# Feed-forward stages: moving a subtraction from GpSimd to VectorE, a rounding from ScalarE to VectorE, and the convolution's input from SBUF to PSUM

## The chip, the cores and the metric

The kernel runs on one core of a Trainium2 chip. The metric is the device time of one execution in microseconds (us), the median over runs. The engines are named as in the profile: PE is TensorE's matmul, PEld its weight load, DVE is VectorE, ACT is ScalarE, POOL is GpSimd, and SP is SyncE, which here only issues loads.

## The reference

A sequence of 256 tokens of width 1024 goes through two transformer layers (an RWKV layer and a differential attention layer, each followed by a dense gated feed-forward) and then through a third block (token mixers with gated linear recurrences, followed by a convolutional gated feed-forward). What matters here are the three feed-forwards:

```python
def swiglu_ffn(h, w_gu, w_down):
    gate, up = jnp.split(h @ w_gu, 2, axis=-1)
    return (jax.nn.silu(gate) * up) @ w_down
...
def conv_ffn(h, w_up, taps, conv_b, w_down, rows):
    a, g = jnp.split(h @ w_up, 2, axis=-1)
    ...
    gc = lax.conv_general_dilated(g2, tp[:, :, None, :].astype(g.dtype), (1, 1), 'SAME', ...
    gc = gc.reshape(bsz, t, f) + conv_b
    return (a * jax.nn.gelu(gc, approximate=False)) @ w_down
```

The dense ones run twice, with 2816 hidden features each. The convolutional one has 2816 hidden features too; its gate branch is a 3x3 depthwise convolution over the 256 tokens seen as a grid of 4 rows of 64.

## The kernel before, in words

**Two-part numbers.** Every operand of a matmul is split into a rounded high part and a low part, `hi` (type fp32r) and `lo = raw - hi`, and each product is three matmuls: high by high, high by low, low by high (`mm3`). `split` (line 276) does this for a tile: ScalarE copies `raw` into `hi` with rounding (line 277), then an engine subtracts (`sub`, line 274). The subtraction runs on VectorE unless the caller names another engine.

**Weights.** `stream` (line 280) loads a weight tile of 128 x 1024 floats (512 KB) with a DMA on SP's queue (`fetch`, line 265) into a ring of five `raw` buffers, and splits it into rings of `hi` and `lo` buffers, three deep each for the up weights, and four deep for the down weights, which are called `dhi` and `dlo` in the profile.

**A feed-forward** (`ffn`) goes over 22 steps `fb` of 128 hidden features. In a step, two weight tiles (f = 0 and f = 1, the gate and the up half) are streamed and 48 matmuls of 256 columns write the two halves of one PSUM bank, which the profile names `p` in two steps and `tr` in the next two. Then `post(fb)` runs a hook that makes the hidden activation `raw` (tile name `act`, 128 x 256), splits it into `acth` and `actl`, and once enough steps are pending streams the down weight of an older step and issues its 12 matmuls of 512 columns into four `acc` banks. So a step has 60 matmuls: 48 and 12. With `lag=2` the down matmuls run two steps behind, and the last four steps' wait until the end (`tail=4`).

**Who subtracts.** The three feed-forwards pass `eng = lambda f: G if f else V` to `ffn`: the `lo` of the f = 0 tile is subtracted on VectorE, that of the f = 1 tile on GpSimd. `dlo` and `actl` are VectorE's.

**The hooks.** `silu_hook` (line 833): ScalarE's Silu of one half of the bank, VectorE's product with the other half (line 836). `conv_hook` (line 1261): ScalarE copies the gate half out of PSUM into a tile `gs` in SBUF (line 1263) and makes the centre tap from it (line 1265); VectorE adds the other eight taps one by one into `cacc` (line 1272), each reading `gs` and `cacc`; ScalarE applies Gelu (line 1274) and VectorE multiplies with the other half of the bank (line 1275).

**Beside the dense feed-forwards** run the modulation vectors of the third block (`ada_extra`): 48 more tiles of 512 KB (`wada`, two buffers, same SP queue), each multiplied and summed on VectorE against one or two rows (tile `junk`, line 856); 20 tiles are asked for in the first dense feed-forward and 28 in the second, and 16 of the 48 are used twice.

**Order.** The instructions of each engine are put in an order by a scheduler that works with its own estimates; each engine then runs its list strictly in that order. So an edit can move instructions far from it, and an instruction that waits holds up all that stand behind it on its engine, loads on SP included.

Of the kernel before, what the change touches and what calls it, by code (L numbers as in the profile page):

```python
# [17 lines left out]
T = 256  # L18
# [149 lines left out]
def body(ctx, tc, a, at):  # L168
# [35 lines left out]
        return scratch("s_" + s, (n + 7) // 8 * 8, 2)[:, :n]  # L204

    class FMt:
        """feature-major [1024, 256]: two tiles of 4 blocks of 128 features"""

        def __init__(self, pool, tag, dt=F32):
            self.t = [pool(tag, 1024, 2, dt) for _ in range(2)]  # L210
# [6 lines left out]
            return self.v[b][:, :, t * P:(t + 1) * P]  # L217

    def mark(*names):
        """the last instruction so far of each of these engines"""  # L220
        own = {getattr(mybir.EngineType, n) for n in names or ("Pool", "Activation", "DVE")}
        m = {}
        for i in reversed(nc.cur_bb.bb.instructions):
            if i.engine in own and i.engine not in m:
                m[i.engine] = i
                if len(m) == len(own):
                    break
        return m
# [26 lines left out]
    def C(n):  # L255
        o, w = at[n]
        return cst[:, o:o + w]
# [115 lines left out]

    def ptm(jobs, hid, lag=2, eng=lambda m: None, acc_bank=lambda: bank("p"),
            gain=None, ring=None):
        """jobs: (weights, first chunk, callback(t, psum)) of 512 output columns each"""
        xh, xl = hid
        steps = [(j, g) for j in range(len(jobs)) for g in range(4)]
        loaded, acc = {}, {}
        for i in range(len(steps) + lag):  # L380
            for t in range(2):
                m = i - lag * t
                if not 0 <= m < len(steps):
                    continue
                j, g = steps[m]
                w, c0, fin = jobs[j]
                if m not in loaded:
                    loaded[m] = stream(w, c0 + g, 2, eng(m), None if gain is None else gain[:, 2 * g:2 * g + 2],
                                       ring)
                wh, wl = loaded[m]  # L390
                if g == 0:
                    acc[j, t] = acc_bank()
                for k in range(2):
                    kk = 2 * g + k
                    tk = slice(t * P, (t + 1) * P)
                    mm3(acc[j, t], xh.k(kk)[:, tk], xl.k(kk)[:, tk], wh[:, k], wl[:, k], kk == 0, kk == 7)
                if g == 3:
                    fin(t, acc[j, t])

    def pfm(w, i, hid, eng=lambda f: None):  # L400
        """two feature-major blocks, in one bank"""
        xh, xl = hid
        ps = bank("p")
        for f in range(2):
            wh, wl = stream(w, 2 * i + f, 8, eng(f))
            for k in range(8):
                mm3(ps[:, f * T:(f + 1) * T], wh[:, k], wl[:, k], xh.k(k), xl.k(k), k == 0, k == 7)
        return ps
# [7 lines left out]
    H = [slice(0, 64), slice(64, 128)]  # L416
    F = [slice(0, T), slice(T, 2 * T)]

# [1 line left out]
    SP, LP, EP = Pool("solve", "right"), Pool("loop", "right"), Pool("early", "right")  # L420
    AP0, XR = Pool("state0"), Pool("xr")
    wa1 = hs(wside("lora1"), P)
# [273 lines left out]
    tps.close()  # L696
    SP.close()

    # state recurrence
    YP, ZP, wps = Pool("yg", "right"), Pool("zt", "right"), Pool("wps", psum=True)  # L700
    Y = tmt(VP, "bvY")
    zt = [ZP("zt", 1024, 3) for _ in range(3)]
# [74 lines left out]
        ptm([(a["w_o"], 4 * n, add_res(n)) for n in range(2)], yg)  # L777
    YP.close()

# [1 line left out]
    def ffn(gu, dn, gain, shift, hook, fin, extra=None, eng=lambda f: None, lag=2, tail=4, then=None):  # L781
        fp_ = Pool("ffn")
        hh_, hl_ = hid = pairHL(fp_, "fh")
# [14 lines left out]
        def post(fb, ps):  # L798
            raw = fp_("act", T, 2)
            hook(fp_, fb, ps, raw)  # L800
            ah, al_ = fp_("acth", T, 7, F32R), fp_("actl", T, 7, F32R)
            split(raw, ah, al_)
            pend.append((fb, ah, al_))
            if len(pend) > lag and NF - 1 - fb + len(pend) > tail:
                f0, ah, al_ = pend.pop(0)
                w = stream(dn, f0, 2, ring=dring)
                for t in range(2):
                    down(f0, t, w, ah, al_)
            if extra:
                with behind(normed if fb < 4 else {}):  # L810
                    extra(fb)
# [23 lines left out]
        S.activation(sl, ps[:, :T], AF.Silu)  # L835
        V.tensor_tensor(out=raw, in0=sl, in1=ps[:, T:], op=ALU.mult)  # L836

    # modulation vectors, a few columns per step of the two dense FFNs
    ada, adc = cp("ada", 48), cp("adc", 16)
    gm = cp("gm", 24).rearrange("p (a k) -> p a k", a=3)  # L840
    HP, DP = Pool("hst"), Pool("ada")
# [15 lines left out]
                                               op1=ALU.add, accum_out=dst[:, e:e + 1])  # L857
        return extra

    ffn(a["gu0"], a["dn0"], C("g_ffn0"), None, silu_hook, add_res, ada_extra(0, 20), lambda f: G if f else V, then=load_c)  # L860

# [1 line left out]
    bad = C("b_ada")  # L863
    V.tensor_tensor(out=adc, in0=adc, in1=bad[:, :16], op=ALU.add)
    V.scalar_tensor_tensor(out=gm[:, 2], in0=adc[:, 8:16], scalar=1.0, in1=C("n_mix"), op0=ALU.add, op1=ALU.mult)
# [127 lines left out]
        sa, sb = nx, cur  # L993
    heads_c(*groups[5], *sb)

# [1 line left out]
    def logsig(pool, ps, g_, k_):  # L997
        t_ = pool("ls", 512, 2)
        S.activation(t_, ps, AF.Abs)
# [55 lines left out]
        CX.close()  # L1055
        cps.close()

    ffn(a["gu1"], a["dn1"], C("g_ffn1"), None, silu_hook, add_res, ada_extra(20, 48), lambda f: G if f else V, then=finish_ctx)
    DP.close()

# [1 line left out]
    GP = Pool("grow")  # L1062
    MX, MH, mps = Pool("mix"), Pool("mh", "right"), Pool("mps", psum=True)
    V.tensor_tensor(out=ada, in0=ada, in1=bad, op=ALU.add)
# [189 lines left out]
    MT.close()  # L1254
    MX.close()

# [1 line left out]
    taps = C("taps").rearrange("p (f k) -> p f k", k=9)  # L1258
    convb = C("convb")

    def conv_hook(fp_, fb, ps, raw):
        gs, acc = fp_("gs", T, 2), fp_("cacc", T, 2)
        S.copy(gs, ps[:, T:])
        g4, a4 = hs(gs, 64), hs(acc, 64)
        S.activation(acc, gs, AF.Identity, scale=taps[:, fb, 4:5], bias=convb[:, fb:fb + 1])  # L1265
        for dy, dx in ((1, 0), (1, 2), (0, 1), (0, 0), (0, 2), (2, 0), (2, 1), (2, 2)):
# [39 lines left out]
```

## Time and profile before

| what | value |
|---|---|
| runs | 1269.65, 1271.04, 1275.42 us; median 1271.04 us |
| span of the profiled execution, first to last instruction | 1265.7 us |
| mean granted TensorE clock | 0.941 |

The profile gives the span of its execution, not a time of its own beside it; the median of the runs is 5.3 us above that span. By stage (busy us of each engine in the stretch, from the view of windows):

| stretch (us) | what runs | PE | DVE | ACT | POOL | granted clock |
|---|---|---|---|---|---|---|
| 257 to 482 | first dense feed-forward, with the end of the RWKV layer | 209.90 | 159.59 | 97.16 | 61.58 | 0.96 |
| 482 to 645 | attention, context states | 155.05 | 104.98 | 105.42 | 44.23 | 0.98 |
| 645 to 863 | second dense feed-forward | 211.29 | 153.76 | 101.87 | 67.11 | 0.98 |
| 863 to 1038 | token mixers | 142.51 | 131.45 | 99.12 | 81.36 | 0.91 |
| 1038 to 1265.7 | convolutional feed-forward and output | 202.20 | 194.32 | 107.66 | 57.71 | 0.96 |

How to read it: a row of the view of groups names line, engine, operation, output <- inputs, shapes and a count, then the busy time in us and the mean in ns of one, then the idle time of the engine in front of them and what ended it. A row of the waits says who waited for whom: us in total, how often, and the longest. A row of the timeline has the start and the duration in us; `x4` is four alike in a row. The chain is the work that ended last, traced backwards. The matmuls' own durations overlap, so the pace of PE is read from the starts.

### The profile page before, as it was taken

The page shows a single profiled execution, that of the slowest core. Times are in us where ns is not written, and L with a number is a line of the kernel's source. Part 1 is how long each engine was busy: PE and PEld are TensorE (multiplying, and loading weights), DVE is VectorE, ACT ScalarE, POOL GpSimd, SP SyncE. Part 2 cuts the span into 40 slices and gives each one's busy share as a digit, 9 for nine tenths or more (in the row PEclk, how much of TensorE's full clock was granted, in tenths as well). Part 3 has the DMA queues.
Part 4 walks back from the last instruction along what each step waited for, and adds up shares of the span by engine and source line. Part 5 has one row for each costly group of instructions (what it writes and reads, how often), then busy time and mean ns, then how long its engine had stood idle before and what let it go on. Part 6 is the DMA issues. An engine that isn't in the chain of part 4 may idle for free.

```text
span 1265.7 us, 19898 instructions
## 1 busy us (share of the span) xinstructions
PE 1136.5 (90%) x7772; PEld 985.2 (78%) x7772; DVE 924.7 (73%) x1384; ACT 645.1 (51%) x1112; POOL 371.7 (29%) x213
## 2 busy tenths in 40 slices
PE   5988889789999999998989999999976889999995
PEld 4877548669888898886678988998954768898884
DVE  5887844858995566856659776564799667998897
ACT  6945143445334356657656434355756355454452
POOL 1323201213222231243143122234268313223221
PEclk8988878889999999999999999999987999999997
DMA  5331110247886563543147886562522244554541
GB/s 183 121 103 48 67 54 35 84 139 249 285 273 227 183 220 110 190 160 126 46 150 264 302 303 229 191 220 95 171 94 83 100 134 155 171 173 151 184 133 50
DMA packets 54573, 198.06 MB, mean 156 GB/s; under 512 B 6064, under 2 KB 6576, under 8 KB 54480
## 3 DMA queue, kind: packets, MB, share of 16 engines
q1 hardware_dynamic: 52128, 189.82, 44.4%
q10 hardware_dynamic: 2352, 6.98, 1.6%
q8 instruction: 61, 1.00, 0.3%
q14 instruction: 32, 0.26, 0.1%
HBM read 195.72 MB, written 1.05 MB: 155 GB/s over the span
## 4 chain that ended last, share of the span: by engine, by line
PE 54%; DVE 19%; issue 12%; ACT 6%; POOL 5%; DMA 3%; POOLq 0%; ACTq 0%; DVEq 0%; SPq 0%
PE p L295 22%; PE tr L295 10%; PE acc L295 8%; PE pj L295 5%; POOL lo L274 4%; DVE cacc L1272 4%; PE sc L295 2%; DVE lo L274 2%; DMA raw<-in_dn 2%; PE W L295 2%; DVE dlo L274 2%; ACT hi L277 1%; PE tr L307 1%; PE v L295 1%; PE px L295 1%
## 5 line engine op out<-in xcount | busy, mean ns | idle before, releaser
L274 POOL TENSOR_TENSOR lo<-raw,hi 128x1024 fp32r<-128x1024 f32 x88 | 237.8, 2703 | 516.9 <-ACT hi L277 474.6
L277 ACT CAST hi<-raw 128x1024 fp32r<-128x1024 f32 x212 | 217.9, 1046 | 68.9 <-PE p L295 35.6
L274 DVE TENSOR_TENSOR lo<-raw,hi 128x1024 fp32r<-128x1024 f32 x124 | 189.2, 1529 | 63.0 <-ACT hi L277 62.8
L295 PE MATMUL p<-fhh,lo 128*128 128x256 f32 x576 | 167.9, 292 | 7.7 <-POOL lo L274 7.0
L295 PE MATMUL p<-fhh,hi 128*128 128x256 f32 x576 | 166.3, 289 | 4.7 <-ACT fhh L358 1.8
L295 PE MATMUL p<-fhl,hi 128*128 128x256 f32 x576 | 166.3, 289 | 1.2 <-DVE fhl L359 0.9
L295 PE MATMUL tr<-fhh,lo 128*128 128x256 f32 x480 | 138.4, 288 | 6.8 <-POOL lo L274 6.8
L295 PE MATMUL tr<-fhh,hi 128*128 128x256 f32 x480 | 137.0, 285 | 0.1
L295 PE MATMUL tr<-fhl,hi 128*128 128x256 f32 x480 | 136.9, 285 | 0.0
L274 DVE TENSOR_TENSOR dlo<-raw,dhi 128x1024 fp32r<-128x1024 f32 x66 | 86.8, 1315 | 65.4 <-ACT dhi L277 65.4
L295 PEld LDWEIGHTS p<-fhh,lo 128*128 128x128 f32 x576 | 113.1, 196 | 10.4 <-POOL lo L274 9.0
L295 PEld LDWEIGHTS p<-fhh,hi 128*128 128x128 f32 x576 | 113.2, 197 | 7.2 <-ACT fhh L358 2.2
L1272 DVE SCALAR_TENSOR_TENSOR cacc<-gs,cst,cacc 128x189 f32<-128x189 f32 (+2 forms) x176 | 114.0, 649 | 4.5 <-ACT cacc L1265 0.3
L295 PEld LDWEIGHTS p<-fhl,hi 128*128 128x128 f32 x576 | 113.2, 197 | 3.2 <-DVE fhl L359 1.5
L277 ACT CAST dhi<-raw 128x1024 fp32r<-128x1024 f32 x66 | 69.2, 1048 | 77.5 <-DMA raw<-in_dn 77.3
L856 DVE CUSTOM_DVE_ANT_0 junk<-wada,crow 128x1024 f32<-128x1024 f32 x64 | 100.8, 1576 | 10.7 <-DMA wada<-in_w_ada 8.3
L295 PE MATMUL acc<-dhi,acth 128*128 128x512 f32 x264 | 104.4, 396 | 4.3 <-ACT acth L277 4.2
L295 PE MATMUL acc<-dhi,actl 128*128 128x512 f32 x264 | 102.0, 395 | 3.0 <-DVE actl L274 2.4
L295 PE MATMUL acc<-dlo,acth 128*128 128x512 f32 x264 | 103.7, 393 | 0.0
L295 PEld LDWEIGHTS tr<-fhh,lo 128*128 128x128 f32 x480 | 93.3, 194 | 8.4 <-POOL lo L274 8.0
L277 ACT CAST acth<-act 128x256 fp32r<-128x256 f32 x66 | 26.7, 405 | 136.8 <-DVE act L836 134.8
L295 PEld LDWEIGHTS tr<-fhh,hi 128*128 128x128 f32 x480 | 93.3, 194 | 1.4 <-ACT hi L277 0.3
(433 smaller groups left out, 2592.9 us busy)
## 6 DMA issues: line engine op xcount, KB each, us to landing
raw<-in_gu SPq DMA_DIRECT2D x132, 512.0 KB, 4.1
raw<-in_dn SPq DMA_DIRECT2D x66, 512.0 KB, 4.2
wada<-in_w_ada SPq DMA_DIRECT2D x48, 512.0 KB, 4.6
raw<-in_w_r SPq DMA_DIRECT2D x8, 512.0 KB, 4.5
raw<-in_w_k SPq DMA_DIRECT2D x8, 512.0 KB, 3.6
raw<-in_w_v SPq DMA_DIRECT2D x8, 512.0 KB, 3.6
raw<-in_w_o SPq DMA_DIRECT2D x8, 512.0 KB, 4.2
raw<-in_w_ak SPq DMA_DIRECT2D x8, 512.0 KB, 4.5
```

The source lines that it names most:

```text
L274: (eng or V).tensor_tensor(out=out, in0=raw, in1=hi.bitcast(F32), op=ALU.subtract)
L277: S.copy(hi, raw)
L295: PE.matmul(out, lhsT=l, rhs=r, start=start, stop=stop, skip_group_check=True)
L307: PE.transpose(o, s_, ident)
L856: V.tensor_tensor_reduce(out=junk, in0=raw, in1=src, scale=1.0, scalar=0.0, op0=ALU.mult, op1=ALU.add, accum_out=dst[:, e:e + 1])
L1272: V.scalar_tensor_tensor(out=a4[:, ro, co], in0=g4[:, ri, ci], scalar=taps[:, fb, k:k + 1], in1=a4[:, ro, co], op0=ALU.mult, op1=ALU.add)
```

## The change

Three edits:

1. The two dense feed-forwards no longer pass `eng`, so VectorE subtracts both tiles of a step; the convolutional one still passes it and keeps GpSimd for f = 1.
2. In `post`, for all three feed-forwards, the high part of the activation is made by VectorE's `tensor_copy` and not by ScalarE's copy; the subtraction behind it was VectorE's already.
3. In `conv_hook` the copy `gs` is gone: ScalarE's centre tap and VectorE's eight other taps read the gate half where the matmuls left it, in PSUM.

Removed comments are left out here.

```diff
             ah, al_ = fp_("acth", T, 7, F32R), fp_("actl", T, 7, F32R)
-            split(raw, ah, al_)
+            V.tensor_copy(ah, raw)
+            sub(V, al_, raw, ah)
...
-    ffn(a["gu0"], a["dn0"], C("g_ffn0"), None, silu_hook, add_res, ada_extra(0, 20), lambda f: G if f else V, then=load_c)
+    ffn(a["gu0"], a["dn0"], C("g_ffn0"), None, silu_hook, add_res, ada_extra(0, 20), then=load_c)
...
-    ffn(a["gu1"], a["dn1"], C("g_ffn1"), None, silu_hook, add_res, ada_extra(20, 48), lambda f: G if f else V, then=finish_ctx)
+    ffn(a["gu1"], a["dn1"], C("g_ffn1"), None, silu_hook, add_res, ada_extra(20, 48), then=finish_ctx)
...
     def conv_hook(fp_, fb, ps, raw):
-        gs, acc = fp_("gs", T, 2), fp_("cacc", T, 2)
-        S.copy(gs, ps[:, T:])
+        gs, acc = ps[:, T:], fp_("cacc", T, 2)
```

The scheduler makes a new order from this. In the list of each engine most changes lie in the three feed-forwards. Three places on VectorE follow; a line number is one higher after the change from `post` on.

VectorE in a late step of the first dense feed-forward, before (`act` is the step's product, `dlo` the low part of a down weight, `lo` that of an up weight):

```order
L836 TENSOR_TENSOR act_3665<-silu_3666,tr_3604 128x256
L274 TENSOR_TENSOR actl_3670<-act_3665,acth_3669 128x256
L274 TENSOR_TENSOR dlo_3949<-raw_3946,dhi_3948 128x1024
L274 TENSOR_TENSOR lo_3881<-raw_3878,hi_3880 128x1024
L836 TENSOR_TENSOR act_3756<-silu_3757,tr_3695 128x256
```

And after, the same step:

```order
L837 TENSOR_TENSOR act_3665<-silu_3666,tr_3604 128x256
L802 CAST acth_3669<-act_3665 128x256
L274 TENSOR_TENSOR actl_3670<-act_3665,acth_3669 128x256
L274 TENSOR_TENSOR dlo_3949<-raw_3946,dhi_3948 128x1024
L274 TENSOR_TENSOR lo_3820<-raw_3817,hi_3819 128x1024
L274 TENSOR_TENSOR lo_3881<-raw_3878,hi_3880 128x1024
L837 TENSOR_TENSOR act_3756<-silu_3757,tr_3695 128x256
```

The f = 1 tile's subtraction (`lo_3820`) has come from GpSimd's list and stands behind `dlo`; the rounding (`acth`) has come from ScalarE's.

VectorE in a step of the convolutional feed-forward, after (before, each tap read `gs`, there was no CAST, and in every second step the two `lo` of two steps stood together):

```order
L1275 TENSOR_TENSOR act_10930<-cacc_10931,p_10869 128x256
L802 CAST acth_10943<-act_10930 128x256
L274 TENSOR_TENSOR actl_10944<-act_10930,acth_10943 128x256
L274 TENSOR_TENSOR lo_11161<-raw_11158,hi_11160 128x1024
L1272 SCALAR_TENSOR_TENSOR cacc_11027<-p_10965,cst_67,cacc_11027 128x4x63 x2
L1272 SCALAR_TENSOR_TENSOR cacc_11027<-p_10965,cst_67,cacc_11027 128x192
L1272 SCALAR_TENSOR_TENSOR cacc_11027<-p_10965,cst_67,cacc_11027 128x3x63
L274 TENSOR_TENSOR dlo_11334<-raw_11331,dhi_11333 128x1024
L1272 SCALAR_TENSOR_TENSOR cacc_11027<-p_10965,cst_67,cacc_11027 128x3x63 x2
L1272 SCALAR_TENSOR_TENSOR cacc_11027<-p_10965,cst_67,cacc_11027 128x192
L1272 SCALAR_TENSOR_TENSOR cacc_11027<-p_10965,cst_67,cacc_11027 128x3x63
L1275 TENSOR_TENSOR act_11026<-cacc_11027,p_10965 128x256
```

Each step now has one `lo`, one `dlo`, eight taps, a product, a rounding and a subtraction.

VectorE in a step of the first dense feed-forward with modulation work, after:

```order
L837 TENSOR_TENSOR act_3032<-silu_3033,tr_2971 128x256
L857 ISA junk_2283,adc_2272<-wada_3331,crow_2282 128x1024
L857 ISA adc_2272 128x1
L802 CAST acth_3036<-act_3032 128x256
L857 ISA junk_2283,ada_2271<-wada_3509,crow_2281 128x1024
L857 ISA ada_2271 128x1
L274 TENSOR_TENSOR actl_3037<-act_3032,acth_3036 128x256
L274 TENSOR_TENSOR lo_3187<-raw_3184,hi_3186 128x1024
L857 ISA junk_2283,adc_2272<-wada_3509,crow_2282 128x1024
L857 ISA adc_2272 128x1
L274 TENSOR_TENSOR dlo_3316<-raw_3313,dhi_3315 128x1024
L274 TENSOR_TENSOR lo_3248<-raw_3245,hi_3247 128x1024
```

Before, this step held four `junk`, one `dlo` and one `lo`; now it holds three `junk`, one `dlo` and two `lo`, and the modulation work reaches some three steps further into the stage.

## Prediction

> **What bounds the kernel now.** I read the page first, then windows around the three feed-forwards, then the waits of PE in them, and last the timeline. The page's head says that PE is busy nearly everywhere and that VectorE is the next one:
>
> ```profile
> span 1265.7 us, 19898 instructions
> PE 1136.5 (90%) x7772; PEld 985.2 (78%) x7772; DVE 924.7 (73%) x1384; ACT 645.1 (51%) x1112; POOL 371.7 (29%) x213
> ```
>
> The change touches only the feed-forwards, so the question is how far each of them stands above PE's own pace. In the chain, an undisturbed step of PE is 48 matmuls and 12 matmuls:
>
> ```profile
> 1096.92 5.75 PE tr L295 x48
> 1102.67 2.75 PE acc L295 x12
> ```
>
> That is 8.50 us a step, or 0.142 us for each of its 60 weight loads. The windows over the even middle of the three stages (columns: length; then busy us and count for PE, PEld, DVE, ACT, POOL; granted clock; DMA share; GB/s) give the real pace:
>
> ```profile
> 308.80:459.60 150.80, 141.85 (x963) 131.71 (x962) 111.62 (x127) 58.13 (x81) 42.52 (x16) 0.98 0.70 234
> 704.90:838.70 133.80, 130.40 (x903) 122.03 (x902) 90.63 (x100) 55.17 (x76) 37.54 (x15) 0.99 0.70 242
> 1093.90:1221.20 127.30, 123.53 (x843) 111.74 (x842) 114.91 (x164) 60.66 (x96) 37.04 (x14) 1.00 0.49 166
> ```
>
> 962 loads are 16.03 steps, 136.3 us at 8.50; the first dense stage spends 150.8, so 14.5 us too many. The second: 902 loads, 15.03 steps, 127.8 us, so 6.0 too many. The convolutional one: 842 loads, 14.03 steps, 119.3 us, so 8.0 too many (9.07 us a step). These are the stocks from which the change can take.
>
> Who makes PE wait differs. The waits of PE in 257 to 482 and of PEld in 1038 to 1262 (us in all, how often, the longest):
>
> ```profile
> PE tr L295 <- POOL lo L274: 4.6, 4, 2.0
> PE p L295 <- POOL lo L274: 4.0, 3, 2.2
> ...
> PEld acc L295 <- DVE actl L274: 7.6, 11, 1.9
> PEld acc L295 <- ACT acth L277: 6.4, 9, 1.7
> ```
>
> In the dense stage it is GpSimd's subtraction, and VectorE's `lo` is never in the list, though it has the same job. In the convolutional stage it is the activation, at the end of VectorE's chain of taps. A stall costs more than its length:
>
> ```profile
> 342.00:362.00 20.00, 19.95 (x143) 18.58 (x141) 19.93 (x26) 7.22 (x11) 5.87 (x3) 1.00 0.79 268
> 362.00:382.00 20.00, 17.88 (x114) 16.82 (x115) 17.32 (x22) 5.72 (x9) 5.91 (x3) 0.91 0.84 285
> ```
>
> After the longest one the granted clock of a 20 us window is 0.91, about 1.8 us of lost clock. So 14.5 us of excess go with only 8.6 us of waits for GpSimd.
>
> **The change, part by part. Contention first,** since all parts lean on it. VectorE and GpSimd in two convolutional steps:
>
> ```profile
> 1157.85 1.23 DVE L274 TENSOR_TENSOR dlo<-raw,dhi 128x1024 fp32r<-128x1024 f32 x1 [0.61 <-ACT dhi L277]
> 1158.85 2.49 POOL L274 TENSOR_TENSOR lo<-raw,hi 128x1024 fp32r<-128x1024 f32 x1 [8.19 <-ACT hi L277]
> 1159.00 3.91 DVE L1272 SCALAR_TENSOR_TENSOR cacc<-gs,cst,cacc 128x189 f32<-128x189 f32 x4
> 1163.45 0.42 DVE L1275 TENSOR_TENSOR act<-cacc,tr 128x256 f32<-128x256 f32 x1 [0.54 <-ACT cacc L1274]
> 1165.87 1.90 DVE L1272 SCALAR_TENSOR_TENSOR cacc<-gs,cst,cacc 128x252 f32<-128x252 f32 x4
> 1167.40 2.62 POOL L274 TENSOR_TENSOR lo<-raw,hi 128x1024 fp32r<-128x1024 f32 x1 [6.06 <-ACT hi L277]
> 1167.68 3.43 DVE L274 TENSOR_TENSOR dlo<-raw,dhi 128x1024 fp32r<-128x1024 f32 x1
> 1171.03 1.76 DVE L1272 SCALAR_TENSOR_TENSOR cacc<-gs,cst,cacc 128x189 f32<-128x189 f32 x4
> ```
>
> Four taps take 1.76 us alone and 3.91 beside GpSimd's subtraction; `dlo` takes 1.23 alone and 3.43 beside it. Whatever VectorE runs then stands still until GpSimd is done, some 2.2 us each time. But not everything. At the start of the second dense stage the same GpSimd subtraction runs beside operations of the taps' very kind that read one input from PSUM:
>
> ```profile
> 656.55 2.40 POOL L274 TENSOR_TENSOR lo<-raw,hi 128x1024 fp32r<-128x1024 f32 x1 [3.81 <-ACT hi L277]
> 656.77 0.61 DVE L359 SCALAR_TENSOR_TENSOR fhl<-tr,cst,fhh 128x128 fp32r<-128x128 f32 x2 [0.98 <-ACT fhh L358]
> ```
>
> Two take 0.61 us inside GpSimd's 2.40: not held. So with the gate half in PSUM, the taps should no longer be held by GpSimd.
>
> **Taps from PSUM.** Groups of the taps before, an operation on 128 columns in SBUF, and two 512-wide operations, without and with a PSUM input:
>
> ```profile
> L1272 DVE SCALAR_TENSOR_TENSOR cacc<-gs,cst,cacc 128x189 f32<-128x189 f32 x88 | 70.6, 802 | 2.3
> L1272 DVE SCALAR_TENSOR_TENSOR cacc<-gs,cst,cacc 128x252 f32<-128x252 f32 x44 | 23.2, 527 | 1.0 <-ACT cacc L1265 0.3
> L1272 DVE SCALAR_TENSOR_TENSOR cacc<-gs,cst,cacc 128x192 f32<-128x192 f32 x44 | 20.4, 465 | 1.2
> L337 DVE TENSOR_SCALAR dg<-cst,s_rstd 128x128 f32<-128x128 f32 x2 | 0.6, 288 | 1.5 <-POOL s_rstd L314 1.5
> L1249 DVE TENSOR_TENSOR xres<-xres,gr 128x512 f32<-128x512 f32 x4 | 2.6, 682 | 0.0
> L1248 DVE TENSOR_TENSOR gr<-acc,grow 128x512 f32<-128x512 f32 x4 | 2.6, 684 | 2.0 <-PE acc L295 2.0
> ```
>
> 682 against 684 ns: PSUM costs nothing that counts, and I take 0 per tap, from the row nearest in kind. An upper bound: the pair at 656.77 took 0.305 each on 128 columns with a PSUM input, 0.017 more than the 0.288 of an SBUF operation on 128 columns (L337), which on 176 taps is 3 us of VectorE. The eight taps of a step cost 114.2 / 22 = 5.19 us now and 1.90 + 1.76 = 3.66 unheld, 1.5 us less. A VectorE step of this stage then is: taps 3.66, `lo` and `dlo` 2 x 1.23, `act` and `actl` 2 x 0.42, the rounding r, and the 0.54 it waits for Gelu: 7.5 + r. [...]
>
> **The rounding on VectorE.** No such SBUF-to-SBUF cast of VectorE is in the trace. Nearest are the one-input operation above, on 128 columns in SBUF, and a copy of 256 columns from PSUM:
>
> ```profile
> L721 DVE COPY zt<-W 64x256 f32<-64x256 f32 x8 | 3.3, 414 | 12.0 <-PE W L295 11.9
> ```
>
> So r lies between 0.29 and 0.41; I take 0.35. It adds 7.7 us of VectorE per stage, but ends a hop to ScalarE and back on the path that made PEld wait above, and ScalarE's list no longer stops at that rounding. VectorE's convolutional step is 7.85 us, against 8.50 for PE: the bound passes to PE, with 0.65 us to spare.
>
> Conv sum: from the first matmul of the stage's step 0 to the last of step 21, the window is
>
> ```profile
> 1045.45:1253.30 207.85, 196.54 (x1320) 178.70 (x1320) 181.33 (x265) 98.87 (x153) 55.89 (x21) 0.98 0.45 150
> ```
>
> 1320 loads are the 22 steps, in 207.9 us, where 22 steps of 8.50 are 187.0: 20.8 too many, 8.0 in the middle and 12.8 at both ends. I take 6 of the 8.0 (2 left for steps that wait for loads) and 5 of the 12.8, since the ends also hold GpSimd's late tiles and the last tap chain, which stay: 11 us.
>
> **Both subtractions on VectorE.** In the late steps of the first dense stage PE is paced by a ring: SP's load of a down weight waits for GpSimd to free its buffer, ScalarE's in-order list waits for that load, and GpSimd waits for ScalarE:
>
> ```profile
> 402.74 0.33 SPq L265 DMA_DIRECT2D raw<-in_dn  x1
> ...
> 407.74 1.05 ACT L277 CAST dhi<-raw 128x1024 fp32r<-128x1024 f32 x1 [3.18 <-DMA raw<-in_dn]
> ...
> 412.32 0.33 SPq L265 DMA_DIRECT2D raw<-in_dn  x1
> ```
>
> The turn takes 9.58 us: 5.00 for the load, 4.58 until the buffer is free. After the change the second part is ScalarE's cast (1.05) and, by the order shown above, `dlo` and `lo` on VectorE (2 x 1.23): 3.5. The turn is 8.5 and PE's pace takes over.
>
> In the early steps VectorE is full (19.93 of 20 us in the window from 342), with modulation work:
>
> ```profile
> 338.33 1.22 DVE L856 CUSTOM_DVE_ANT_0 junk<-wada,crow 128x1024 f32<-128x1024 f32 x1
> ```
>
> Four `junk`, `dlo` and `lo`, `act` and `actl` were 4 x 1.22 + 2 x 1.23 + 2 x 0.42 = 8.2 us a step, and one hold of 2.2 beside GpSimd makes 10.4. Now three `junk` stand in a step, three subtractions, `act`, `actl` and the rounding: 3 x 1.22 + 3 x 1.23 + 2 x 0.42 + 0.35 = 8.5 us, with no hold. That equals PE's 8.50: VectorE is no longer late by more than a little, but has nothing to spare while modulation work lasts.
>
> Dense sum: of 14.5 us in the first stage I take 10 away (the waits for GpSimd, 8.6, with some of the clock lost behind them; the rest stays as VectorE's small lateness), of 6.0 in the second 4.
>
> What I cost at nothing: the copies and roundings taken from ScalarE (busy 58.13 of 150.80 us and 60.66 of 127.30, so they shorten nothing by themselves); the 1.23 us subtractions put on VectorE in the late dense steps, hidden behind PE's 8.50 since VectorE holds there only 3 x 1.23 + 2 x 0.42 + 0.35 = 4.9 us a step; and the PSUM bank, which is held to the same end, since L1275 read it last before too. If the cover in the early steps fails, by 0.3 us in each of some ten steps, that is 3 us, which the 4.5 left in place allow for.
>
> Sum: 10 + 4 + 11 = 25 us. The profiled span goes from 1265.7 to 1240.7; the median stands 5.3 above that span, so it goes from 1271.0 to 1246.
>
> **The rivals.** *The dense stages gain nothing*: VectorE, full in the early steps, is late by as much as GpSimd was. For it: 8.5 against 8.50. Against: the hold of 2.2 goes. Then only the 11 remain: 1260.
>
> *The convolutional stage gains nothing*: GpSimd's `lo`, which no longer holds the taps, now holds `dlo` or `lo`, at 3.43 for 1.23. For it: the row at 1167.68. If that met every step, VectorE's step would be 7.85 + 2.2 = 10.05, over PE's 8.50, and worse than now; against it, a held `dlo` only delays a tile that is needed later, and VectorE's 0.65 us to spare catches up. I price it as no gain: 1271 - 14 = 1257. [...]
>
> *Nothing helps*: PE's excess comes from the clock and the loads, and the waits removed come back as others: 1271.
>
> *Slower*: the `lo` of f = 1 now stands behind `dlo` on VectorE's list, and `dlo` waits for ScalarE. VectorE's waits in 257 to 482 and in 645 to 863:
>
> ```profile
> DVE dlo L274 <- ACT dhi L277: 29.2, 13, 3.8
> ...
> DVE dlo L274 <- ACT dhi L277: 32.8, 16, 3.8
> ```
>
> Those are 62 us in 29 waits, 2.1 each. GpSimd used to subtract its tile whatever VectorE waited for; now that tile waits too. If half of it reaches PE, that is +31, the 14 of the dense stages are lost, and with 11 from the convolutional stage the time is 1271 + 31 - 11 = 1291. For it: the order shown above. Against it: the `lo` of f = 0 stands behind the same waits already, and PE's list of waits has no VectorE `lo` in it. It decides from the point at which a tile's `lo` is made less than 2.1 us before PE needs it, in most late steps.
>
> **How the numbers follow.** My forecast, 0.58: 1246, on its own 1236 (all but 6 of the stocks of 14.5, 6.0 and 20.8 us) to 1257 (the 5 us at the convolution's ends don't come, the taps cost their upper 3, the early dense steps 3 more). Dense without gain 0.12, convolution without gain 0.12, nothing 0.09, slower 0.09. A measurement of this kernel can tell about 0.5%, 6.4 us, from no change. The first three cases are faster by more: 0.82; within it 0.09; slower 0.09. The range leaves out the last two cases and reaches past the second and third: 1234 to 1263.
>
> **What would show it in the profile after.** The rows of PE waiting for GpSimd's `lo` are gone in the first dense stage, and its 16 steps of the middle take near 140 us with the clock at 1.00 where it was 0.91. Taps of 189 columns take near 0.42 us each and not 802 ns, also beside GpSimd. The 22 convolutional steps take about 197 us. If PE waits for VectorE's `lo` in the dense stages, the slower rival is right; if `dlo` stands at 3.4 beside GpSimd in most convolutional steps and PEld waits for `actl` still, the third case is; if PE's excess stays with neither wait in its list, my reading of who paces it is wrong.

## The result, and the profile after

The changed kernel takes 1233.4 us (median of 4 runs, 1230.0 to 1237.0) against 1270.4 before (median of 4 runs beside it): ratio 0.9687, 95% interval 0.9656 to 0.9719. The forecast of 1246 had the direction right, but the gain is 37 us and not 25, and the time lies just under the lower end of the range, 1234.

The page of the changed kernel; its profiled execution has a span of 1231.1 us, so the median stands 2.3 us above it (before: 5.3):

```profile
span 1231.1 us, 19845 instructions
PE 1121.4 (91%) x7772; PEld 976.5 (79%) x7772; DVE 889.7 (72%) x1494; ACT 618.8 (50%) x1026; POOL 252.1 (20%) x169
```

VectorE has 44 subtractions and 66 roundings more to do (1494 instructions for 1384), and yet its busy time falls by 35 us: the time in which it is held counts as busy (four taps held beside GpSimd stood with 3.91 us before, four beside it now with 1.76). Where the time went shows in the three stages, each cut from its first up matmul to its last down matmul. Windows of before (the convolutional one was shown, 207.85 in a cut 0.4 us longer), then of after; columns as in the prediction:

```profile
281.75:484.29 202.54, 193.59 (x1321) 180.20 (x1320) 149.41 (x176) 87.08 (x125) 58.07 (x21) 0.98 0.69 231
659.93:863.50 203.57, 197.32 (x1349) 183.38 (x1349) 144.27 (x166) 93.81 (x135) 57.56 (x25) 0.98 0.70 243
1045.47:1252.87 207.40, 196.10 (x1319) 178.51 (x1320) 180.88 (x265) 98.86 (x153) 55.89 (x21) 0.98 0.45 150
```

```profile
281.51:469.21 187.70, 187.70 (x1321) 176.45 (x1320) 144.38 (x219) 80.84 (x104) 0.00 (x0) 1.00 0.74 250
647.61:842.63 195.02, 193.72 (x1349) 180.25 (x1349) 141.11 (x210) 90.31 (x117) 3.71 (x4) 1.00 0.74 252
1024.04:1218.29 194.25, 189.74 (x1319) 177.37 (x1320) 152.58 (x287) 83.28 (x109) 52.14 (x21) 0.99 0.49 160
```

22 steps of 8.50 are 187.0. The first dense stage takes 187.70: PE is busy in all of it. The chain of after shows it step by step; the starts are 8.50 us apart, here at the beginning and at the end of the stage:

```profile
302.90 5.75 PE tr L295 x48
311.40 5.75 PE p L295 x48
319.90 5.75 PE p L295 x48
...
430.40 5.75 PE tr L295 x48
438.90 5.75 PE tr L295 x48
```

All steps in the middle of the other two stages have the same 8.50. The waits of PE in 257 to 482 of after all lie outside the stage (from 281 to 470 there is none); GpSimd's 4.6 and 4.0 us are gone, and VectorE's `lo` has not come in their place:

```profile
PE tr L295 <- DVE fhl L359: 3.8, 1, 3.8
PE tr L295 <- DVE dg L337: 2.3, 1, 2.3
PE p L295 <- DVE xres L413: 0.3, 1, 0.3
PE pj L295 <- ACT xnh L277: 0.2, 1, 0.2
```

The prediction's claim on the taps is in the timeline of VectorE and GpSimd in one convolutional step of after:

```profile
1110.20 1.22 DVE L274 TENSOR_TENSOR lo<-raw,hi 128x1024 fp32r<-128x1024 f32 x1
1111.33 1.89 DVE L1272 SCALAR_TENSOR_TENSOR cacc<-p,cst,cacc 128x252 f32<-128x252 f32 x4
1114.23 1.23 DVE L274 TENSOR_TENSOR dlo<-raw,dhi 128x1024 fp32r<-128x1024 f32 x1 [1.00 <-ACT dhi L277]
1115.37 1.76 DVE L1272 SCALAR_TENSOR_TENSOR cacc<-p,cst,cacc 128x189 f32<-128x189 f32 x4
```

```profile
1115.22 2.49 POOL L274 TENSOR_TENSOR lo<-raw,hi 128x1024 fp32r<-128x1024 f32 x1 [6.12 <-ACT hi L277]
```

Four taps take 1.76 us in the middle of GpSimd's 2.49; before, four beside it took 3.91. The group of 189 columns has a mean of 413 ns where it had 802.

### The profile page after: what moved, and what is told of

Read it like the earlier page. It is cut to its first block, busy times and chain, and to the rows that moved or that the text cites. A ratio compares the mean times of both kernels' runs of the same rounds, so it can differ in the third digit from the quotient of the medians.

```text
span 1231.1 us, 19845 instructions
## 1 busy us (share of the span) xinstructions
PE 1121.4 (91%) x7772; PEld 976.5 (79%) x7772; DVE 889.7 (72%) x1494; ACT 618.8 (50%) x1026; POOL 252.1 (20%) x169
## 4 chain that ended last, share of the span: by engine, by line
PE 68%; DVE 15%; ACT 7%; issue 4%; DMA 3%; POOL 3%; POOLq 0%; ACTq 0%; DVEq 0%; SPq 0%
PE p L295 27%; PE tr L295 14%; PE acc L295 13%; PE pj L295 5%; PE sc L295 3%; DMA raw<-in_dn 2%; DVE lo L274 2%; PE W L295 2%; ACT hi L277 2%; POOL lo L274 1%; DVE cacc L1272 1%; PE tr L307 1%; DVE dlo L274 1%; PE px L295 1%; PE v L295 1%
## 5 line engine op out<-in xcount | busy, mean ns | idle before, releaser
L274 DVE TENSOR_TENSOR lo<-raw,hi 128x1024 fp32r<-128x1024 f32 x168 | 212.4, 1270 | 69.4 <-ACT hi L277 69.1
L295 PE MATMUL p<-fhh,lo 128*128 128x256 f32 x576 | 163.8, 284 | 0.0
L274 POOL TENSOR_TENSOR lo<-raw,hi 128x1024 fp32r<-128x1024 f32 x44 | 117.4, 2671 | 204.2 <-ACT hi L277 196.4
L295 PE MATMUL tr<-fhh,lo 128*128 128x256 f32 x480 | 135.7, 283 | 0.0
L274 DVE TENSOR_TENSOR dlo<-raw,dhi 128x1024 fp32r<-128x1024 f32 x66 | 84.0, 1273 | 63.9 <-ACT dhi L277 63.6
L314 POOL TENSOR_TENSOR s_rstd<-s_ms,mhalf 128x1 f32<-128x1 f32 (+2 forms) x32 | 35.6, 1115 | 346.5 <-DVE s_ms L328 272.4
L295 PEld LDWEIGHTS tr<-fhl,hi 128*128 128x128 f32 x480 | 92.0, 192 | 1.2 <-issue 0.2
L857 DVE CUSTOM_DVE_ANT_0 junk<-wada,crow 128x1024 f32<-128x1024 f32 x64 | 78.2, 1222 | 8.5 <-DMA wada<-in_w_ada 7.0
```

What stands on the lines that cost most here:

```text
L274: (eng or V).tensor_tensor(out=out, in0=raw, in1=hi.bitcast(F32), op=ALU.subtract)
L295: PE.matmul(out, lhsT=l, rhs=r, start=start, stop=stop, skip_group_check=True)
L314: G.tensor_tensor(out=r, in0=ms, in1=mhalf[:, :n], op=ALU.pow)
L857: V.tensor_tensor_reduce(out=junk, in0=raw, in1=src, scale=1.0, scalar=0.0, op0=ALU.mult, op1=ALU.add, accum_out=dst[:, e:e + 1])
```

## The experiments

All ratios are to the kernel before, run beside each on the same chip, where its median was 1270.4 to 1274.4 us. The stages are cut as above, each in one profiled execution.

| kernel | median us | ratio, 95% interval | dense 1 | dense 2 | conv |
|---|---|---|---|---|---|
| before | 1270.35 | | 202.5 | 203.6 | 207.4 |
| changed | 1233.41 | 0.9687 (0.9656 to 0.9719) | 187.7 | 195.0 | 194.3 |
| first edit only | 1249.92 | 0.9811 (0.9787 to 0.9835) | 187.7 | 194.9 | 209.3 |
| second edit only | 1276.41 | 1.0026 (1.0004 to 1.0047) | 202.6 | 209.2 | 209.5 |
| third edit only | 1261.40 | 0.9907 (0.9873 to 0.9940) | 205.8 | 206.9 | 195.2 |
| second and third | 1258.76 | 0.9887 (0.9857 to 0.9917) | 203.5 | 208.5 | 193.8 |
| first and second | 1251.02 | 0.9824 (0.9795 to 0.9853) | 187.7 | 194.9 | 211.0 |
| changed + idle GpSimd subtraction | 1261.34 | 0.9893 (0.9866 to 0.9921) | 202.3 | 207.0 | 192.8 |
| changed + idle GpSimd memsets | 1234.14 | 0.9680 (0.9647 to 0.9712) | 187.7 | 195.3 | 192.9 |
| changed, conv without GpSimd | 1229.11 | 0.9654 (0.9628 to 0.9680) | 187.7 | 195.0 | 188.2 |
| the same, taps from SBUF | 1227.76 | 0.9646 (0.9622 to 0.9671) | 187.7 | 195.0 | 188.8 |
| before, feed-forwards without GpSimd | 1229.44 | 0.9649 (0.9617 to 0.9681) | 187.7 | 195.9 | 190.3 |
| the same, taps from PSUM | 1227.21 | 0.9631 (0.9596 to 0.9665) | 187.7 | 194.9 | 189.8 |
| before, no `lo` on GpSimd but two at the start | 1218.51 | 0.9570 (0.9538 to 0.9601) | 187.7 | 192.2 | 192.0 |

**One edit at a time.** The first edit alone is the kernel before with these two lines:

```diff
-    ffn(a["gu0"], ..., ada_extra(0, 20), lambda f: G if f else V, then=load_c)
+    ffn(a["gu0"], ..., ada_extra(0, 20), then=load_c)
-    ffn(a["gu1"], ..., ada_extra(20, 48), lambda f: G if f else V, then=finish_ctx)
+    ffn(a["gu1"], ..., ada_extra(20, 48), then=finish_ctx)
```

> The kernel before with only the first edit: VectorE subtracts all up-weight tiles of the two dense feed-forwards; rounding and taps as before. Theory (GpSimd's late tile and its hold on VectorE are all that kept PE above 8.50 us a step in the dense stages): the two stages come down to what they take in the changed kernel, 187.7 and 195.0 us from 202.6 and 203.6, the convolutional one stays at 207: about 1247 us (1244 to 1252). Rival (VectorE is the bound there and the rounding's place matters as well): 1258 or more, with PE waiting for VectorE's lo or ScalarE's acth.

The theory held to the tenth in the dense stages, 187.7 and 194.9, and the time is 1249.9, in the range given. With GpSimd out of them, the rounding's place makes no difference to the dense stages.

The second edit alone:

```diff
-            split(raw, ah, al_)
+            V.tensor_copy(ah, raw)
+            sub(V, al_, raw, ah)
```

> The kernel before with only the second edit: the activation is rounded on VectorE in all three feed-forwards. Theory (the rounding adds 0.29 us to a VectorE that is held and late, and takes a hop away; the two nearly cancel): 1270 us, between 1266 and 1273. Rival (the hop to ScalarE and back is what made PE wait for the activation in the convolutional stage, 7.6 and 6.4 us of waits): 1257 to 1263.

Neither: it is 0.26% slower, and 1276 lies above both ranges. The waits of PEld in its convolutional stage have changed their name and not their size:

```profile
PEld acc L295 <- DVE acth L802: 9.8, 13, 1.8
...
PEld acc L295 <- DVE actl L274: 3.2, 13, 1.0
```

13.0 us in all, against 14.0 before (`actl` 7.6 and `acth` 6.4). So with the hop to ScalarE gone PE waits as long for the end of VectorE's chain. The longer time comes from the second dense stage (209.2 for 203.6) and the convolutional one (209.5 for 207.4); why the second dense stage is longer was not tried.

The third edit alone:

```diff
-        gs, acc = fp_("gs", T, 2), fp_("cacc", T, 2)
-        S.copy(gs, ps[:, T:])
+        gs, acc = ps[:, T:], fp_("cacc", T, 2)
```

> The kernel before with only the third edit: the taps read the gate half in PSUM, no copy. Theory (GpSimd's hold on the taps is what made VectorE's convolutional step longer than PE's): taps of 189 columns go from 802 to about 420 ns, the stage comes down by 9 to 13 us, total 1257 to 1262. Rival (the hop of the rounding is as much to blame): 4 to 6 us, 1265.

1261.4, as the theory had it; the stage comes down by 12.2 us. Its dense stages read 205.8 and 206.9, some 3 us more than before each, though every engine has the same order of instructions there: the first stage, with VectorE held in it (before, the mean of its `lo` in 257 to 482 is 1847 ns, and 1222 in the changed kernel's 301.5 to 450), took 202.5 us in one execution and 205.8 in the other. The five kernels of the table that have a GpSimd subtraction there (the one before and the one with the idle subtraction among them) give 202.3 to 205.8 us in the first stage and 203.6 to 209.2 in the second; those without give 187.7 each time, and 192.2 to 195.9.

**Two edits.** The changed kernel with the first edit undone:

> The changed kernel with the first edit undone: GpSimd subtracts f = 1 in the dense stages again; rounding and taps as changed. Theory (the stages are independent): the dense stages go back to about 202 and 203 us, the convolutional one stays at 194: about 1257 us (1254 to 1260). Rival (the rounding on VectorE eases the dense stages too): 1250 or less.

1258.8: as expected, and the dense stages are back at 203.5 and 208.5. With the third undone instead (the copy and the taps from it are back):

> The changed kernel with only the third edit undone: the copy into SBUF is back and GpSimd subtracts f = 1 in the convolutional stage. Theory (the hold on the taps is the cost): taps of 189 columns at 800 ns on the mean again, the convolutional stage at 203 to 209 us for 194, total 1243 to 1248. Rival (the rounding's hop was the cost and is gone): 1233 to 1237.

The theory was right in the main, and too mild: 1251.0, and the convolutional stage, 211.0, is longer than before the change. VectorE's steps there, from one `lo` to the next, alternate between about 9.65 and 9.73 us. GpSimd's subtraction meets the taps of 189 columns in every second step only (their mean is 630 ns and not 800) and `dlo` in the others (mean 1852 ns). The stage takes 1.7 us more than with the first edit alone (209.3); that this is the rounding's 0.29 us a step is likely, but not shown.

**Hold or lateness.** In the dense stages two explanations were left: GpSimd's tile came late to PE, or GpSimd held VectorE. This kernel is the changed one with a GpSimd subtraction in each dense step that nobody waits for:

```diff
+        idle = fp_("idle") if extra else None
...
+                if extra and f:
+                    wf = wh.rearrange("p k c -> p (k c)").bitcast(F32)
+                    G.tensor_tensor(out=idle, in0=wf, in1=wf, op=ALU.subtract)
```

> The changed kernel, with one more GpSimd subtraction in each step of the dense feed-forwards, of the same size as the one that was taken away (hi of the f = 1 tile minus itself, into a tile that nobody reads). So VectorE can be held again, but no tile that PE needs comes late from GpSimd. Theory A (the hold was the cost): VectorE's 7.3 us a step in the early part become 9.5, over PE's 8.50, about 13 us in the first stage and up to 5 in the second: 1245 to 1252. Theory B (the late GpSimd tile was the cost, the hold is hidden behind PE): 1233 to 1237, with VectorE's subtractions at 3.4 us where they meet GpSimd.

By the time it is theory A: 1261.3, the dense stages 202.3 and 207.0, so as much as the first edit gained is lost, and no tile that PE needs comes from GpSimd. (The idle subtraction also reads `hi` and so keeps its buffer; ScalarE waited for that once in each stage, 2.2 us.) It cost more than the 18 us of the expectation, since the second stage lost 12.0. The waits of PE in 257 to 490 and VectorE's groups in 301.5 to 450 of this kernel:

```profile
PE tr L295 <- DVE lo L274: 6.2, 3, 4.0
...
PE p L295 <- DVE lo L274: 2.5, 4, 1.0
```

```profile
L274 DVE TENSOR_TENSOR lo<-raw,hi 128x1024 fp32r<-128x1024 f32 x33 | 51.7, 1575 | 0.0
L861 DVE CUSTOM_DVE_ANT_0 junk<-wada,crow 128x1024 f32<-128x1024 f32 x33 | 45.9, 1390 | 0.0
L274 DVE TENSOR_TENSOR dlo<-raw,dhi 128x1024 fp32r<-128x1024 f32 x17 | 24.1, 1420 | 13.3 <-ACT dhi L277 13.3
```

Now it is VectorE that is late, 8.7 us of waits for its `lo`, with the means of 1.22 us grown to 1.39 to 1.58. An inserted instruction also gives another order, so a control has GpSimd work at the same places, paced by the same tile, but writing only:

```diff
-                    G.tensor_tensor(out=idle, in0=wf, in1=wf, op=ALU.subtract)
+                    w1 = wh[:, 0, :1].bitcast(F32)
+                    G.tensor_tensor(out=idle[:, :1], in0=w1, in1=w1, op=ALU.subtract)
+                    for _ in range(2):
+                        G.memset(idle, 0.0)
```

> A control for the idle GpSimd subtraction: the changed kernel with GpSimd working at the same places of the dense feed-forwards, paced by the same tile (one element per partition is read), but otherwise only writing: two memsets of 128 x 1024. Theory (what holds VectorE is GpSimd reading SBUF beside an operation of VectorE that reads two SBUF tiles): next to no hold, 1232 to 1238 us. Rival (any GpSimd work there, or the other order of instructions that an inserted one brings, costs what the idle subtraction cost): 1252 to 1262.

1234.1, no different from the changed kernel. Its GpSimd groups in 301.5 to 450, and VectorE's `lo` there:

```profile
L826 POOL MEMSET idle<- 128x1024 f32 x35 | 33.5, 956 | 2.0
L824 POOL TENSOR_TENSOR idle<-hi 128x1 f32<-128x1 f32 x17 | 13.6, 797 | 97.6 <-ACT hi L277 97.6
```

```profile
L274 DVE TENSOR_TENSOR lo<-raw,hi 128x1024 fp32r<-128x1024 f32 x36 | 43.9, 1221 | 12.2 <-ACT hi L277 12.2
```

GpSimd is busy for 47 us of 148.5, more than with the idle subtraction (38), and VectorE's `lo` stays at 1221 ns. So it is not GpSimd's being busy that costs: its subtraction, which reads SBUF, holds VectorE's operations with two SBUF inputs (`lo`, `dlo` and `junk` at means of 1.39 to 1.58 us), and its memsets, which only write, do not (1.22 us). Of the 70 `lo`, `dlo` and `junk` that stand beside a memset in this kernel none takes over 1.23 us. (For the rounding, which has one input, see the last section.)

That the first stage comes back to 202.3 us, where it was 202.5 before the change, is partly chance, since the loss lies elsewhere. In the ten early steps from 304.37 to 401.34, with modulation work, the kernel with the idle subtraction spends 96.97 us where ten of 8.50 are 85.0, and VectorE is busy for 93.55 of them. For the late steps, without modulation work, here are the windows of the changed kernel with the first edit undone, with PE's waits in it, and of the one with the idle subtraction:

```profile
388.39:463.03 74.64, 69.53 (x482) 64.38 (x480) 42.72 (x47) 28.47 (x36) 19.37 (x8) 1.00 0.59 195
```

```profile
PE p L295 <- POOL lo L274: 3.5, 3, 2.0
PE tr L295 <- POOL lo L274: 1.4, 2, 1.0
```

```profile
411.06:462.67 51.61, 51.50 (x361) 48.15 (x360) 38.17 (x40) 20.71 (x25) 11.47 (x6) 1.00 0.62 204
```

The first are 8 steps, 6.6 us over 8.50 each (the kernel before spends 72.37 us on 8 such steps, 4.4 over). The second are 6 steps, only 0.6 us over, and PE waits for nothing in them, although VectorE's `lo` is held there too (mean 1739 ns). So theory A holds for the early steps, where VectorE has no 2.2 us to spare. In the late steps VectorE can bear the hold, and what cost time there was the late tile of GpSimd, theory B.

**GpSimd out of the convolutional stage.** The changed kernel, with `eng` dropped in the third call too, and the same with the copy into SBUF back:

```diff
-    ffn(a["gu2"], ..., lambda n: gated_res(1, n), None,
-        lambda f: G if f else V)
+    ffn(a["gu2"], ..., lambda n: gated_res(1, n), None)
```

> The changed kernel with VectorE subtracting both tiles in the convolutional feed-forward as well, so GpSimd subtracts nothing there; taps from PSUM. Theory (VectorE's own work decides, with nobody to hold it): a step is 3.66 of taps, 3 x 1.23, 2 x 0.42 and 0.29, that is 8.5 us, or 9.0 with its wait for Gelu, against PE's 8.50: between 1233 and 1243. Rival (what GpSimd still holds, some dlo and lo at 2.4 to 3.1 us, is a cost worth more than the work): 1229 to 1232.

> As the kernel above (VectorE subtracts everything in the convolutional stage), but with the copy of the gate half into SBUF back, so that the taps read SBUF with no GpSimd subtraction beside them. Theory (the place of the gate half matters only because of GpSimd): taps of 189 columns near 420 ns, the time within 3 us of the kernel above. [...]

In the first the rival won: 1229.1 and a stage of 188.2, although VectorE has 22 x 1.22 = 27 us more to do. The work fits: in 1080 to 1200 VectorE is busy for 106.69 of 120 us, 7.6 a step and not 8.5 (the part on why the prediction missed says why), and PE all the time:

```profile
1080.00:1200.00 120.00, 120.00 (x848) 113.03 (x847) 106.69 (x207) 54.70 (x71) 0.00 (x0) 1.00 0.51 169
```

The 6 us against the changed kernel lie at the stage's ends. In the first 20 us of the changed kernel's stage the granted clock is 0.91, and here 1.00; in the second 20 us, where an `actl` of VectorE takes 2.61 us beside GpSimd, PE is busy for 18.18 us, and here for all. In the last 20 us of the changed kernel's stage a `dlo` of VectorE stands beside GpSimd's last subtraction, and PE, which then waits 2.3 us for `acth`, is busy for 17.66 us; here PE is busy for all of the last 20. The `dlo` of the changed kernel:

```profile
1199.80 3.09 DVE L274 TENSOR_TENSOR dlo<-raw,dhi 128x1024 fp32r<-128x1024 f32 x1
```

In the second, the theory held: 1227.8, and the taps take the same from SBUF as from PSUM:

```profile
L1273 DVE SCALAR_TENSOR_TENSOR cacc<-gs,cst,cacc 128x189 f32<-128x189 f32 x88 | 35.6, 411 | 1.5
```

411 ns here, 409 and 410 in the two groups of the kernel before it. Here, reading from PSUM was worth something only beside GpSimd (413 ns for a tap of 189 columns in the changed kernel, 802 before).

**Without the second and third edit.** The kernel before, with `eng` dropped in all three feed-forwards and nothing else changed; and that with the third edit:

> The kernel before with one edit only: VectorE subtracts both up-weight tiles in all three feed-forwards; the rounding stays on ScalarE and the taps read the copy in SBUF. Theory (GpSimd's hold is the whole cost, and the second and third edit matter only beside it): every stage at PE's 8.50 us a step, 1226 to 1231 us, within 3 us of the two kernels without GpSimd in the convolutional stage. Rival (rounding and PSUM reading each bring something of their own): 1234 or more, with PE waiting for ScalarE's acth.

> As the kernel above, with the third edit too (taps from PSUM, no copy on ScalarE); the rounding stays on ScalarE. Theory: 1226 to 1231 us, no measurable difference from the one above. Rival (the copy is on the path): faster by 3 us or more than the one above.

1229.4 and 1227.2, with intervals that overlap each other and those of the two kernels above. With GpSimd gone, the second and third edit have nothing left to bring that these runs can tell.

**GpSimd out of nearly all.** PE waits once for 7.5 us in the token mixers for a GpSimd `lo` in the kernel without GpSimd in its feed-forwards:

```profile
PE p L295 <- POOL lo L274: 7.5, 1, 7.5
```

So the last kernel drops `eng` in the context projections and the token mixers too, and GpSimd's share of a `split` of activations in the RWKV layer (two subtractions of weights at the program's start stay on GpSimd, unlike what the expectation says):

```diff
-    ptm([(a["w_iv"], 0, lambda t, ps: S.copy(cv[:, t * 512:(t + 1) * 512], ps))], ch, 0, lambda m: G)
+    ptm([(a["w_iv"], 0, lambda t, ps: S.copy(cv[:, t * 512:(t + 1) * 512], ps))], ch, 0)
...
-        ptm([(w, 0, got.__setitem__)], ch, 0, lambda m: G, acc_bank=acc_bank)
+        ptm([(w, 0, got.__setitem__)], ch, 0, acc_bank=acc_bank)
...
-        eng=lambda m: G if m % 2 else V)
```

> The kernel before with VectorE subtracting every weight tile of the whole program, GpSimd none (feed-forwards, context projections, token mixers), rounding and taps as before. Theory (PE's 7.2 us wait for a GpSimd lo in the token mixers goes, and holds elsewhere): 5 to 12 us under the kernel with VectorE in the feed-forwards alone, 1215 to 1224. Rival (VectorE bounds the mixers, 136 of 181 us busy there): no gain, 1226 to 1235.

1218.5: the stretch between the second dense and the convolutional stage comes down from 182.33 to 172.97 us, and this is the fastest kernel of the study, 0.957 of the time before. The windows, of the kernel with VectorE in the feed-forwards alone and of this one:

```profile
840.19:1022.52 182.33, 147.23 (x1268) 125.15 (x1266) 136.54 (x161) 103.72 (x158) 79.97 (x50) 0.91 0.34 111
```

```profile
840.63:1013.60 172.97, 146.71 (x1267) 124.29 (x1265) 133.44 (x168) 104.59 (x158) 54.95 (x42) 0.94 0.37 117
```

VectorE is busy for less time there, with more subtractions to do. The wait of 7.5 us is gone (PE waits 2.7 us for VectorE's `lo` now), and the granted clock of the stretch is 0.94 for 0.91.

## Why the prediction missed

The sum, term by term, in the profiled executions:

| term | forecast | measured | from |
|---|---|---|---|
| first dense stage | -10 | -14.8 | 202.54 to 187.70 |
| second dense stage | -4 | -8.6 | 203.57 to 195.02 |
| convolutional stage | -11 | -13.2 | 207.40 to 194.25 |
| the rest of the program | 0 | +1.9 | 652.2 to 654.1 |
| median above the span | 0 | -3.0 | 5.3 to 2.3 |
| sum | -25 | -37.6 | 1271.0 to 1233.4 |

**The mechanism was right, and its sizes were not.** The prediction has two costs in the dense stages, a VectorE that is full and held in the early steps, and a late GpSimd tile in the late ones, and one in the convolutional stage, the held taps. The idle subtraction and its control show the first. Its late steps, beside those in which PE needs GpSimd's tile, show the second, and the third edit alone shows the third. With all three gone PE's 8.50 took over. Two things are not shown: that the late tile came from the ring of loads and buffers that the prediction describes, and how the loss of the early steps before was shared between the hold and the late tile.

**First dense stage: the 4.5 us kept back were not there.** The step that failed is the size of VectorE's early step, "3 x 1.22 + 3 x 1.23 + 2 x 0.42 + 0.35 = 8.5 us", and what was drawn from it, "VectorE is no longer late by more than a little, but has nothing to spare". The count of three `junk` a step was right: there are 33 in the 11 steps from 299.88 on. But VectorE is busy for 85.70 us in these steps, which is 7.8 a step:

```profile
299.88:393.38 93.50, 93.50 (x663) 88.10 (x662) 85.70 (x135) 36.83 (x44) 0.00 (x0) 1.00 0.86 291
```

```profile
L857 DVE CUSTOM_DVE_ANT_0 junk<-wada,crow 128x1024 f32<-128x1024 f32 x33 | 40.3, 1222 | 0.3
```

The durations of VectorE's instructions overlap, as those of the matmuls do (from 311.36 in the changed kernel, one of 256 columns stands with 0.28 us and the next starts 0.11 to 0.12 us later). Three in a row, in a step of this stage:

```profile
317.56 1.22 DVE L274 TENSOR_TENSOR dlo<-raw,dhi 128x1024 fp32r<-128x1024 f32 x1
318.70 1.22 DVE L274 TENSOR_TENSOR lo<-raw,hi 128x1024 fp32r<-128x1024 f32 x1
319.83 0.41 DVE L837 TENSOR_TENSOR act<-silu,p 128x256 f32<-128x256 f32 x1
```

From one start to the next a subtraction takes 1.14 us and not 1.22, and a sum of durations counts the overlap twice. So some 0.7 us a step were to spare, and nothing had to be kept back. (Single steps were full, with 8.50 us of VectorE in the 8.50 from 299.88, but PE waits for nothing in the stage.) The same slip is in the 8.5 us a step that was expected for the convolutional stage without GpSimd.

**Second dense stage: the stock was mis-sized.** I counted 6.0 us too many in the even middle, took 4 of it, and gave the ends nothing. Every step of the middle is at 8.50 now, so all of the 6.0 went. The other 2.6 came from the ends, which a cut at the first and last matmul would have shown, as it did for the convolutional stage: 203.57 against 187.0, 16.6 too many (with 29 matmuls of other work among them).

**Convolutional stage.** The middle gave all of its 8.0 and not 6: every step there is at 8.50, none is left that waits for loads. The ends gave 5.2, as taken (5).

**The rounding.** "Ends a hop to ScalarE and back on the path that made PEld wait" brought nothing: the second edit alone is 0.04 to 0.47% slower, and with GpSimd out of the feed-forwards it makes no difference that these runs can tell. Its own price was near, 0.29 us for the 0.35 taken.

**The median.** That it stands above the span by the same 5.3 us was taken over from before. In the four timed runs of the changed kernel the time stands 2.1 to 2.2 us above the span. By that difference, as an estimate, the profiled execution of before took 1268 us, just under the shortest of its timed runs (1268.9): it was a short one, and 3 of the 5.3 us were the distance from it to the median. The profiled execution of after (1233.3) lies in the middle of its timed runs.

**The rivals.** "The dense stages gain nothing" and "the convolutional stage gains nothing" failed by their stages. Of the second the mechanism was half true: GpSimd does hold `dlo` and `lo` now (means of 1378 and 1335 ns), but only twice each, and all four within 41 us of the stage's ends, where some 6 us were lost; in the middle its subtraction stands beside the taps. The slower rival failed where the text had put its test: PE's waits in the dense stages name no `lo` of VectorE, though VectorE's waits for `dhi` go on in the first of them (17.0 us after, for 29.2).

## What to carry to other kernels

An engine that helps can cost more than its help: before giving GpSimd a share of VectorE's work, look at what VectorE's instructions take while GpSimd runs, and price the hold (here 2.2 us) against the work saved (1.22 us). The hold cost time where the held engine had none to spare (12.0 us in the ten early steps, 0.6 in the six late ones); where it has, look at whether the helper's own result comes late. Taking the neighbour that holds an engine away was worth more here than making single operations immune to it (a convolutional stage of 190.3 us for 207.4, against 195.2 with the taps from PSUM). Count the stock of a stage from its first to its last matmul, not only in the even middle. And price an engine's step by its busy time or from start to start: a sum of durations that overlap made an engine look full here that was not (8.5 us a step for 7.8).

## What the runs showed of the hardware

**A one-input operation can be held as well.** The theory that the control tried has the hold for operations that read two SBUF tiles. With the second edit alone, VectorE's rounding from SBUF to SBUF met GpSimd's subtraction three times and took 2.05 to 2.50 us for 0.29. In the kernel with the idle subtraction, VectorE and GpSimd at 450:

```profile
450.13 1.53 DVE L803 CAST acth<-act 128x256 fp32r<-128x256 f32 x1
```

```profile
449.48 2.04 POOL L824 TENSOR_TENSOR idle<-hi 128x1024 f32<-128x1024 f32 x1 [1.93 <-ACT hi L277]
```

The rounding ends some 0.15 us after GpSimd.

The memsets of the control held the rounding too, though none of the 70 `lo`, `dlo` and `junk` beside one took over 1.23 us. Of the seven roundings that stand beside one, the three that began after it took 0.56, 0.83 and 1.06 us, and the four that began before it took 0.28 to 0.29. The longest, and the two memsets it met:

```profile
743.92 1.06 DVE L803 CAST acth<-act 128x256 fp32r<-128x256 f32 x1
```

```profile
742.87 1.97 POOL L826 MEMSET idle<- 128x1024 f32 x2
```

It ends 0.14 us after the second memset. In all it cost the control nothing that its time can tell.

**The clock.** The rest of the program lost 1.9 us. The stretch between the two dense stages, where no instruction was edited, takes 178.4 us after and 175.6 before. In both kernels the granted clock falls there, where PE has pauses (one window of 10 us with 6.51 us of PE in each). It falls to the same depth, 0.50, but for a different time. The windows of before, and of after:

```profile
579.89:583.30 3.41, 3.41 (x14) 3.03 (x13) 0.93 (x3) 3.41 (x16) 2.19 (x1) 0.50 0.33 130
603.78:607.18 3.40, 3.40 (x5) 0.88 (x5) 2.29 (x8) 2.40 (x11) 1.52 (x2) 0.50 0.00 0
```

```profile
585.76:599.41 13.65, 12.61 (x28) 6.82 (x28) 7.90 (x21) 6.26 (x20) 1.71 (x2) 0.50 0.00 2
```

At half the clock, as an estimate from these windows, the two of before lose 3.4 us and the one of after 6.8. The 3.4 us between them are more than the 2.8 by which the stretch is longer. The kernel before with GpSimd out of its feed-forwards has one such window of 3.4 us in this stretch, and there it takes 173.9 us. What sets the length of such a fall was not tried and stays open.
